# Two trunk layers on one core: the last pieces of layer 0 and the first of layer 1 taken in twos, block by block, with a third buffer for the modulation weights

## The chip, the cores and the metric

The kernel runs on one core of a Trainium2 chip, in fp32 with matmuls on fp32r halves. The metric is the time on the device in microseconds (us), the median of a few runs; lower is better.

## The reference, cut to what matters

Two layers are computed for 128 context tokens and 256 latent tokens, which share all weights. Each layer first derives a shift, a scale and a gate from a condition vector, then norms and modulates its input, projects it, mixes it, projects it back and adds it through the gate.

```python
def _rmsnorm(x, g):
    y = xf * lax.rsqrt(jnp.mean(xf * xf, axis=-1, keepdims=True) + NORM_EPS)
    ...
def _adaln(cond, w_mod, b_mod):
    m = jax.nn.silu(cond) @ w_mod + b_mod          # (2048) @ (2048, 6144)
    return jnp.split(m, 3, axis=-1)                # shift, scale, gate
def _modulate(x, norm_g, shift, scale):
    return _rmsnorm(x, norm_g) * (1.0 + scale) + shift
...
for layer in range(DEPTH):
    h_p = _modulate(y_prompt, norm_g, sh_p, sc_p)  # context tokens: c_ctx
    h_s = _modulate(y_sample, norm_g, sh_s, sc_s)  # latent tokens: c
    # layer 0: h @ l0_w_in (7680 columns), HGRN2 scans and attention, @ l0_w_out
    # layer 1: h @ l1_w_in (5120 columns), windowed attention, @ l1_w_out
    y_prompt = y_prompt + gt_p * out_p
    y_sample = y_sample + gt_s * out_s
```

## The kernel before, in words

All 384 tokens are kept on the chip as three blocks of 128: block 0 is the context, blocks 1 and 2 are the latent tokens. A fp32 product is made from halves: a value is split into a rounded part (`hi`, `hh`) and the rest (`lo`, `hl`), and three matmuls replace one (L334 to L341).

`group` multiplies one column group of a weight matrix with all tokens. It walks over the 2048 rows of the weights in pieces of 512 KB: 2 row tiles by 512 columns, or 4 by 256, so 8 or 4 pieces a group. `w_piece` loads a piece on SyncE's queue into `raw` (4 buffers, L315), ScalarE rounds it to `whi` (3 buffers, L317), and VectorE subtracts to get `wlo` (2 buffers, L319). Then TensorE runs the piece's matmuls, block of tokens by block of tokens, into one PSUM tile per block; a group with token rows has 3 blocks x row tiles x 3 matmuls. A block's sum is complete only in the last piece. After every piece, `step` runs one step of the queued work on heads, and `pump` runs some units of the modulation work.

A unit of modulation work is one row tile of `l*_w_mod`: a load of 128 x 1024 floats into `mraw` (2 buffers, SyncE's queue, L229) and two VectorE operations that add its rows, times the condition, into `acc` (L233, L235). Eight such sums run through the kernel, 16 units each, 128 units in all.

The order on each engine is fixed before the run, by a list scheduler: of the instructions that its own clock holds ready, an engine gets the one of highest priority. The order of the program is the priority, and `tc.high_priority(n)` moves instructions ahead by `n`; `w_piece` has BOOST. Engines then run their lists in order, and wait where the data is not there.

The layer change is the place where layer 0's output projection ends and layer 1's input projection begins. The output projection goes over five column groups (`COLS`): three of 512 and two of 256 columns. In each group, a block's sum is multiplied by the gate (L994), the residual is added (L997), ScalarE squares and sums it (`sum_sq`, L361), the result goes to DRAM for later (`y1d`, L999, on GpSimd's queue), and TensorE turns it to feature-major tiles (`turn_x`, L368) that ScalarE scales (L977). After the last group, `rstd_row` makes 1/rms for each block: a VectorE sum (L382) and scaling (L373), a power on GpSimd (L374), a turn on TensorE (L385) into one PSUM tile `rb1`. `modulate_scaled` then makes `h1` in four quarters of 4 row tiles: for quarter 0, row tile by row tile, VectorE multiplies by `rb1` block by block (L412, tile tE), ScalarE adds the shift and rounds (`hh`, L416), VectorE makes the rest (`hl`, L417). Quarters 1 to 3 (tiles tF, tG, tH) are made by `next_h1`, with multiplies over two row tiles and all tokens; quarter 1 ahead of layer 1's first group, quarter 2 after that group's second piece, quarter 3 after its fourth. That first group is 512 columns wide (keys, `k1`), and each of its 8 pieces uses half a quarter. In this text W0, W1, W2 are its first three pieces.

Of the kernel before, what the change touches and what calls it, by code (L numbers as in the profile page):

```python
# [14 lines left out]
P = 128  # L15
# [20 lines left out]
MRAWB = 2  # L36
# [8 lines left out]
def trunk_kernel(ctx: ExitStack, tc: tile.TileContext, I, O):  # L45
# [177 lines left out]
    def mod_acc(l, c0):  # L223

        acc = mpool.tile([P, 2, 1024], F32, tag="acc", name=nm("acc"))
        cs = csil_g[l] if c0 >= 2 * D else csil
        for kt in range(KT):
            raw = wpool.tile([P, 1024], F32, tag="mraw", bufs=MRAWB, name=nm("mraw"))
            nc.sync.dma_start(raw, I[f"l{l}_w_mod"][kt * P:kt * P + P, c0:c0 + 1024])  # L229
# [92 lines left out]
    def group(w, c0, hq, fm, after=None, n=512):  # L322

        nt = 4 if fm else 3
        nk = 1024 // n
        ps = [psm.tile([P, 512], F32, tag="mm", name=nm("mm"))[:, 0:T if fm else n] for _ in range(nt)]
        for kt in range(0, KT, nk):
            hh, hl = hq[kt // 4]
            with tc.high_priority(BOOST):
                hi, lo = w_piece(wpool, "raw", RAWB, w, kt, nk, c0, n)  # L330
            for c in range(nt):
                cs = slice(c * P, c * P + P)
                for k in range(nk):
                    kq = kt % 4 + k  # L334
                    if fm:
                        ops = ((hi[:, k, cs], hh[:, kq]), (hi[:, k, cs], hl[:, kq]), (lo[:, k, cs], hh[:, kq]))
                    else:
                        ops = ((hh[:, kq, cs], hi[:, k]), (hh[:, kq, cs], lo[:, k]), (hl[:, kq, cs], hi[:, k]))
                    for i, (a, b) in enumerate(ops):
                        nc.tensor.matmul(ps[c], lhsT=a, rhs=b, start=(kt + k == 0 and i == 0),  # L340
                                         stop=(kt + k == KT - 1 and i == 2))  # L341
# [9 lines left out]
    def group_b(w, c0, hq, n=512):  # L351
        return group(w, c0, hq, False, n=n)
# [5 lines left out]
    def sum_sq(ss, x, g):  # L358
        for b in range(3):
# [45 lines left out]
    def modulate_scaled(l, q, xt, rb, parts):  # L405

        hh, hl = hq_tiles(q)
        for k0, k1, cts in parts:
            for c, s in cts:
                x = xt[:, k0:k1, s]  # L410
                r = rb[:, s].unsqueeze(1).broadcast_to([P, k1 - k0, s.stop - s.start])
                nc.vector.tensor_tensor(out=x, in0=x, in1=r, op=ALU.mult)  # L412
            for k in range(k0, k1):
                for c, s in CT if len(cts) == 1 else cts:
# [256 lines left out]
    def start_mod(k0, k1):  # L671

        for k, nk in pairs(k0, k1):
# [18 lines left out]
            sums = small(4 * nk, "ms").rearrange("p (b c) -> p b c", c=2)  # L692
# [286 lines left out]
    COLS = [(512 * g, 512) for g in range(3)] + [(1536, 256), (1792, 256)]  # L979
    for i, (c0, n) in enumerate(COLS):  # L980
        g, o = c0 // 512, c0 % 512
        if o == 0:
            x = load_x("CD"[g % 2], g, nc.gpsimd)
        ps = group_b(I["l0_w_out"], c0, o0, n)
# [7 lines left out]
        with tc.high_priority(2 * BOOST if i == 4 else BOOST):  # L992
            for b in range(3):
                nc.vector.tensor_tensor(out=y[:, b], in0=ps[b], in1=gb[:, min(b, 1), o:o + n], op=ALU.mult)  # L994
        with tc.high_priority(2 * BOOST if i == 4 else 0):
# [6 lines left out]
        if i < 4:  # L1002
            later(0, turn)
        else:
            with tc.high_priority(2 * BOOST):
                turn()


    finish_mods()
    h1 = []  # L1010
    ALL = ((0, slice(0, T)),)
    BLOCKS = ((0, slice(0, P)), (1, slice(P, 2 * P)), (1, slice(2 * P, T)))

    def next_h1(q):
        with tc.high_priority(BOOST):
            h1.append(modulate_scaled(1, q, yT[q], rb1, ((0, 2, ALL), (2, 4, ALL))))

    with tc.high_priority(2 * BOOST):
        rb1 = rstd_row(ss1)
# [129 lines left out]
```

## Time and profile before

| what | value |
|---|---|
| median of 3 runs | 1389.26 us (1388.11 to 1390.78) |
| profiled execution, its own time | 1387.91 us |
| span in its trace | 1386.1 us |
| TensorE busy (matmuls) | 1336.0 us, 96% of the span |
| VectorE busy | 1022.0 us, 74% |
| ScalarE busy | 651.6 us, 47% |
| DMA | 265.45 MB, mean 192 GB/s |

The profile is of one execution. A matmul's end is modelled and consecutive matmuls overlap, so busy time of TensorE says little about how densely they follow each other; the distance between two starts says more. An idle time in a row is that of the engine just before the instruction, with what ended it. The granted clock is given as a share of 2.4 GHz.

### The profile page before, as it was taken

The page shows a single profiled execution, that of the slowest core. Times are in us where ns is not written, and L with a number is a line of the kernel's source. Part 1 is how long each engine was busy: PE and PEld are TensorE (multiplying, and loading weights), DVE is VectorE, ACT ScalarE, POOL GpSimd, SP SyncE. Part 2 cuts the span into 40 slices and gives each one's busy share as a digit, 9 for nine tenths or more (in the row PEclk, how much of TensorE's full clock was granted, in tenths as well). Part 3 has the DMA queues.
Part 4 walks back from the last instruction along what each step waited for, and adds up shares of the span by engine and source line. Part 5 has one row for each costly group of instructions (what it writes and reads, how often), then busy time and mean ns, then how long its engine had stood idle before and what let it go on. Part 6 is the DMA issues. An engine that isn't in the chain of part 4 may idle for free.

```text
span 1386.1 us, 19705 instructions
## 1 busy us (share of the span) xinstructions
PE 1336.0 (96%) x7381; PEld 1148.0 (83%) x7381; DVE 1022.0 (74%) x1608; ACT 651.6 (47%) x1302; POOL 80.6 (6%) x86
## 2 busy tenths in 40 slices
PE   5899999999999999999999998989999999999998
PEld 4778788987888887788977896878888899997788
DVE  6587658998996999984896357885656664488753
ACT  4532324485654545655432345434866763352221
POOL 1000000000000041101000000200000001000000
PEclk8999999999999999999999998999999999999999
DMA  9899898746554475665577542674322335457742
GB/s 285 276 347 326 289 304 288 228 128 221 162 187 133 153 226 189 212 215 168 158 237 243 180 149 88 220 250 139 105 78 91 96 113 173 132 174 224 242 163 69
DMA packets 142239, 265.45 MB, mean 192 GB/s; under 512 B 8960, under 2 KB 54976, under 8 KB 142144
## 3 DMA queue, kind: packets, MB, share of 16 engines
q1 hardware_dynamic: 136288, 245.73, 55.2%
q0 software_dynamic: 5600, 18.39, 4.4%
q8 instruction: 58, 0.95, 0.3%
q14 instruction: 37, 0.30, 0.1%
q10 hardware_dynamic: 256, 0.08, 0.0%
HBM read 256.04 MB, written 8.13 MB: 191 GB/s over the span
## 4 chain that ended last, share of the span: by engine, by line
PE 73%; DVE 12%; DMA 9%; issue 3%; POOL 1%; ACT 1%; SPq 0%; DVEq 0%; POOLq 0%; ACTq 0%
PE mm L340 49%; DMA mraw<-in_l_w_mod_dram 8%; DVE acc L235 5%; PE mm L661 4%; PE mm L663 4%; PE mm L662 4%; DVE wlo L319 3%; PE px L519 3%; PE px L682 2%; DMA raw<-in_l_w_in_dram 1%; PE px L579 1%; POOL sm L374 1%; PE px L596 1%; PE px L542 1%; PE px L368 1%
## 5 line engine op out<-in xcount | busy, mean ns | idle before, releaser
L317 ACT CAST whi<-raw 128x1024 fp32r<-128x1024 f32 (+1 forms) x270 | 278.1, 1031 | 527.6 <-PE mm L340 399.8
L319 DVE TENSOR_TENSOR wlo<-raw,whi 128x1024 fp32r<-128x1024 f32 (+1 forms) x270 | 323.6, 1199 | 190.9 <-PE mm L340 152.2
L340 PE MATMUL mm<-wlo,hh 128*128 128x512 f32 (+1 forms) x1104 | 414.3, 375 | 13.4 <-DVE wlo L319 13.4
L340 PE MATMUL mm<-whi,hh 128*128 128x512 f32 (+1 forms) x1104 | 418.3, 379 | 1.2 <-ACT hh L416 0.8
L340 PE MATMUL mm<-whi,hl 128*128 128x512 f32 (+1 forms) x1104 | 413.1, 374 | 0.0
L235 DVE SCALAR_TENSOR_TENSOR acc<-mraw,csil,acc 128x1024 f32<-128x1024 f32 x240 | 301.6, 1282 | 39.0 <-DMA mraw<-in_l_w_mod_dram 38.5
L340 PEld LDWEIGHTS mm<-wlo,hh 128*128 128x128 f32 x1104 | 209.7, 190 | 53.3 <-DVE wlo L319 19.3
L340 PEld LDWEIGHTS mm<-whi,hh 128*128 128x128 f32 x1104 | 209.4, 190 | 39.2 <-issue 1.7
L340 PEld LDWEIGHTS mm<-whi,hl 128*128 128x128 f32 x1104 | 209.6, 190 | 36.1
L661 PE MATMUL mm<-hh,whi 128*128 128x384 f32 x384 | 132.8, 352 | 7.5 <-ACT hh L401 4.4
L340 PE MATMUL mm<-hh,whi 128*128 128x384 f32 x384 | 131.5, 342 | 1.3 <-DVE tM L612 1.3
L662 PE MATMUL mm<-hl,whi 128*128 128x384 f32 x384 | 130.9, 341 | 0.1
L340 PE MATMUL mm<-hh,wlo 128*128 128x384 f32 x384 | 129.5, 337 | 0.0
L340 PE MATMUL mm<-hl,whi 128*128 128x384 f32 x384 | 129.1, 336 | 0.0
L663 PE MATMUL mm<-hh,wlo 128*128 128x384 f32 x384 | 125.2, 342 | 1.1 <-DVE wlo L319 1.1
L661 PEld LDWEIGHTS mm<-hh,whi 128*128 128x128 f32 x384 | 73.3, 192 | 21.4 <-issue 10.4
L663 PEld LDWEIGHTS mm<-hh,wlo 128*128 128x128 f32 x384 | 73.1, 192 | 3.4 <-DVE wlo L319 1.7
L340 PEld LDWEIGHTS mm<-hh,whi 128*128 128x128 f32 x384 | 72.2, 188 | 3.4 <-DVE tM L612 2.2
L662 PEld LDWEIGHTS mm<-hl,whi 128*128 128x128 f32 x384 | 73.7, 192 | 0.8 <-DVE hl L402 0.4
L340 PEld LDWEIGHTS mm<-hl,whi 128*128 128x128 f32 x384 | 72.2, 188 | 0.9
L340 PEld LDWEIGHTS mm<-hh,wlo 128*128 128x128 f32 x384 | 72.1, 188 | 0.7 <-issue 0.2
L554 ACT ACTIVATE p<-px,nb,rs 128x384 f32<-128x384 f32 (+1 forms) x72 | 42.3, 594 | 13.0 <-DVE nb L552 8.3
(445 smaller groups left out, 1404.9 us busy)
## 6 DMA issues: line engine op xcount, KB each, us to landing
raw<-in_l_w_in_dram SPq DMA_DIRECT2D x194, 512.0 KB, 4.0
mraw<-in_l_w_mod_dram SPq DMA_DIRECT2D x192, 512.0 KB, 4.9
raw<-in_l_w_out_dram SPq DMA_DIRECT2D x64, 512.0 KB, 4.4
raw<-in_l_w_in_dram SPq DMA_DIRECT2D x12, 256.0 KB, 7.2
tK<-in_l_b_mod_dram POOLq DMA_DIRECT2D x6, 256.0 KB, 5.6
y1d<-tA POOLq DMA_DIRECT2D x2, 768.0 KB, 6.5
tD<-y1d POOLq DMA_DIRECT2D x2, 768.0 KB, 6.3
tL<-y1d POOLq DMA_DIRECT2D x2, 768.0 KB, 6.7
```

The source lines that it names most:

```text
L235: nc.vector.scalar_tensor_tensor(out=acc[:, c], in0=raw, scalar=s, in1=acc[:, c], op0=ALU.mult, op1=ALU.add)
L317: nc.scalar.copy(hi, raw)
L319: nc.vector.tensor_tensor(out=lo, in0=raw, in1=hi.bitcast(F32), op=ALU.subtract)
L340: nc.tensor.matmul(ps[c], lhsT=a, rhs=b, start=(kt + k == 0 and i == 0), stop=(kt + k == KT - 1 and i == 2))
L368: nc.tensor.transpose(ps[:, b * P:b * P + P], x[:, b, k * P:k * P + P], ident)
L374: nc.gpsimd.tensor_tensor(out=out, in0=out, in1=nhalf[:, 0:out.shape[1]], op=ALU.pow)
L519: nc.tensor.matmul(out, lhsT=a, rhs=b, start=(i == 0), stop=(i == len(ops) - 1))
L554: nc.scalar.activation(p[:, j], ss[j], AF.Exp, bias=nb[:, j:j + 1], scale=rs[:, i + j:i + j + 1], accum_out=sm[:, j:j + 1])
L661: nc.tensor.matmul(ps[c][:, 0:T], lhsT=wh, rhs=hh[:, kq], start=(kt + k == k0), stop=False)
L662: nc.tensor.matmul(ps[c][:, 0:T], lhsT=wh, rhs=hl[:, kq], start=False, stop=False)
L663: nc.tensor.matmul(ps[c][:, 0:T], lhsT=wl, rhs=hh[:, kq], start=False, stop=(kt + k == k1 - 1))
L682: nc.tensor.matmul(ps[32 * (j % 4):32 * (j % 4) + 32, part * n:part * n + n], lhsT=cs32[:, kt, :], rhs=raw[:, j], start=(kt < 4), stop=(kt ...
```

## The change

The buffers of `mraw` go from 2 to 3, and `mod_acc` issues each load two units ahead of its use (one more `yield` per sum). `group` gets an argument `two`: a piece in it is held, and its matmuls are run together with those of the next piece, block by block: all of both pieces for block 0, then for block 1, then for block 2, with the products of `lo` weights last in each piece and block. It is used for the third and fourth piece of the last column group of layer 0 and for the first and second piece of layer 1. The work after a block of the last column group (gate, residual, square, norm) is made per block at a higher priority, and quarter 0 of `h1` block by block. Each block has a PSUM tile of its own for the turned norm, and ScalarE copies it to a tile in SBUF for the later quarters. The last store to `y1d` goes to SyncE's queue. A small tile (`ms`) moves to another pool.

```diff
-MRAWB = 2
+MRAWB = 3
...
 def mod_acc(l, c0):
+        raws = []
+        def load(kt):
+            raws.append(wpool.tile([P, 1024], F32, tag="mraw", bufs=MRAWB, name=nm("mraw")))
+            nc.sync.dma_start(raws[kt], I[f"l{l}_w_mod"][kt * P:kt * P + P, c0:c0 + 1024])
+        for kt in range(MRAWB - 1):
+            load(kt)
+        yield
         for kt in range(KT):
-            raw = wpool.tile([P, 1024], F32, tag="mraw", bufs=MRAWB, name=nm("mraw"))
-            nc.sync.dma_start(raw, I[f"l{l}_w_mod"][kt * P:kt * P + P, c0:c0 + 1024])
+            if kt + MRAWB <= KT:
+                load(kt + MRAWB - 1)
+            raw = raws[kt]
...
-    def group(w, c0, hq, fm, after=None, n=512):
+    def group(w, c0, hq, fm, after=None, n=512, two=()):
+        def products_of(c, kt, hi, lo):
+            ...
+            if held:
+                ops = [o for i, o in enumerate(ops) if i % 3 != 1] + ops[1::3]
+            for i, (a, b) in enumerate(ops):
+                nc.tensor.matmul(ps[c], lhsT=a, rhs=b, start=(kt == 0 and i == 0),
+                                 stop=(kt + nk == KT and i == len(ops) - 1))
+        held = []
         for kt in range(0, KT, nk):
...
+            if kt // nk in two:
+                held.append((kt, hi, lo))
+            else:
+                if held:
+                    held.append((kt, hi, lo))
+                for c in range(nt):
+                    for p in held or ((kt, hi, lo),):
+                        products_of(c, *p)
+                held.clear()
...
-            sums = small(4 * nk, "ms").rearrange("p (b c) -> p b c", c=2)
+            sums = spool.tile([P, 8], F32, tag="ms", bufs=2, name=nm("ms"))[:, 0:4 * nk].rearrange("p (b c) -> p b c", c=2)
...
+    def norm_block(b):
+        r = r1[:, b:b + 1]
+        nc.vector.tensor_reduce(out=r, in_=ss1[:, b:b + 1], axis=AX.X, op=ALU.add)
+        rpow(r, r, D, EPS)
+        ps = px()
+        nc.tensor.transpose(ps[:, 0:P], r.broadcast_to([P, P]), ident)
+        return ps[:, 0:P]
+
+    def first_h1(b, rb):
+        s, c = slice(b * P, b * P + P), min(b, 1)
+        for k in range(4):
+            x, m = yT[0][:, k, s], modc[1][:, k, c:c + 1]
+            nc.vector.tensor_tensor(out=x, in0=x, in1=rb, op=ALU.mult)
+            nc.scalar.activation(h1[0][0][:, k, s], x, AF.Identity, bias=m)
+            nc.vector.scalar_tensor_tensor(out=h1[0][1][:, k, s], in0=x, scalar=m, in1=h1[0][0][:, k, s].bitcast(F32),
+                                           op0=ALU.add, op1=ALU.subtract)
...
     for i, (c0, n) in enumerate(COLS):
+        last = i == len(COLS) - 1
-        ps = group_b(I["l0_w_out"], c0, o0, n)
+        ps = group_b(I["l0_w_out"], c0, o0, n, (2,) if last else ())
...
+        for b in range(3):
+            with tc.high_priority(3 * BOOST if last else BOOST):
                 nc.vector.tensor_tensor(out=y[:, b], in0=ps[b], in1=gb[:, min(b, 1), o:o + n], op=ALU.mult)
+            if last:
+                with tc.high_priority(3 * BOOST):
+                    nc.vector.tensor_tensor(out=y[:, b], in0=y[:, b], in1=xo[:, b], op=ALU.add)
+                    sum_sq(ss1, y, i, (b,))
+                    rb = norm_block(b)
+                with tc.high_priority(2 * BOOST):
+                    first_h1(b, rb)
+                    nc.scalar.copy(rb1[:, b * P:b * P + P], rb)
...
-        nc.gpsimd.dma_start(y1d[:, c0:c0 + n].rearrange("(b p) c -> p b c", p=P), y)
+        (nc.sync if last else nc.gpsimd).dma_start(y1d[:, c0:c0 + n].rearrange("(b p) c -> p b c", p=P), y)
...
-            with tc.high_priority(2 * BOOST):
+            with tc.high_priority(BOOST):
                 turn()
...
-    with tc.high_priority(2 * BOOST):
-        rb1 = rstd_row(ss1)
-        h1.append(modulate_scaled(1, 0, yT[0], rb1, [(k, k + 1, BLOCKS) for k in range(4)]))
...
-    evict_tm(group(W1, 2048, h1, False, lambda q: next_h1(q + 2) if q < 2 else None), k1)
+    evict_tm(group(W1, 2048, h1, False, lambda q: next_h1(q + 2) if q < 2 else None, two=(0,)), k1)
```

## Rows read from the trace of the kernel before

**Rows 1.** The page: busy time of each engine, share of the span, instructions

```profile
PE 1336.0 (96%) x7381; PEld 1148.0 (83%) x7381; DVE 1022.0 (74%) x1608; ACT 651.6 (47%) x1302; POOL 80.6 (6%) x86
```

**Rows 2.** TensorE's waits over the span: us in total, times, longest us

```profile
PE mm L340 <- DVE wlo L319: 13.4, 11, 3.2
```

**Rows 3.** VectorE's waits over the span, the same columns

```profile
DVE acc L235 <- DMA mraw<-in_l_w_mod_dram: 38.5, 35, 4.6
```

**Rows 4.** Windows: length; busy us of PE, PEld, DVE, ACT, POOL; clock; DMA share; GB/s

```profile
0.00:100.00 100.00, 78.51 (x585) 63.73 (x586) 67.00 (x128) 42.15 (x88) 4.18 (x11) 0.91 0.93 300
...
736.80:740.20 3.40, 3.38 (x8) 2.71 (x9) 2.69 (x3) 0.00 (x0) 0.00 (x0) 0.51 0.78 263
...
838.00:842.50 4.50, 4.45 (x11) 3.52 (x12) 4.45 (x19) 3.18 (x9) 0.00 (x0) 0.50 0.09 33
...
852.20:856.40 4.20, 4.18 (x11) 3.32 (x12) 4.20 (x10) 1.85 (x5) 0.00 (x0) 0.59 0.43 125
...
865.00:935.00 70.00, 66.33 (x297) 53.59 (x296) 62.11 (x59) 25.46 (x51) 9.21 (x3) 1.00 0.72 234
```

**Rows 5.** Timeline of TensorE at the layer change: start, us, line, operation [idle before]

```profile
823.18 0.28 PE L340 MATMUL mm<-whi,hl 128*128 128x256 f32 x1
...
826.06 0.28 PE L340 MATMUL mm<-whi,hl 128*128 128x256 f32 x1
...
832.82 0.28 PE L340 MATMUL mm<-whi,hl 128*128 128x256 f32 x1
...
838.05 0.80 PE L340 MATMUL mm<-whi,hh 128*128 128x512 f32 x1 [0.81 <-ACT hh L416]
...
843.03 0.40 PE L340 MATMUL mm<-whi,hh 128*128 128x512 f32 x1
...
848.25 0.39 PE L340 MATMUL mm<-whi,hl 128*128 128x512 f32 x1
...
852.22 0.51 PE L340 MATMUL mm<-wlo,hh 128*128 128x512 f32 x1 [2.90 <-DVE wlo L319]
```

**Rows 6.** Timeline of VectorE at the layer change

```profile
828.90 0.42 DVE L994 TENSOR_TENSOR tB<-mm,tM 128x256 f32<-128x256 f32 x1 [0.28 <-PE mm L340]
...
833.02 1.22 DVE L319 TENSOR_TENSOR wlo<-raw,whi 128x1024 fp32r<-128x1024 f32 x1 [0.42 <-PE mm L340]
834.16 0.42 DVE L994 TENSOR_TENSOR tB<-mm,tM 128x256 f32<-128x256 f32 x1
...
837.27 0.68 DVE L412 TENSOR_TENSOR tE<-tE,px 128x128 f32<-128x128 f32 x3 [1.26 <-PE px L385]
...
842.64 0.95 DVE L412 TENSOR_TENSOR tF<-tF,px 128x768 f32<-128x768 f32 x1
845.99 0.65 DVE L417 SCALAR_TENSOR_TENSOR hl<-tE,modc,hh 128x128 fp32r<-128x128 f32 x2 [2.40 <-ACT hh L416]
...
850.93 1.23 DVE L319 TENSOR_TENSOR wlo<-raw,whi 128x1024 fp32r<-128x1024 f32 x1
```

**Rows 7.** Timeline of SyncE's queue and of VectorE in layer 0's output projection

```profile
725.08 0.34 SPq L229 DMA_DIRECT2D mraw<-in_l_w_mod_dram  x1
...
733.15 2.48 DVE L235 SCALAR_TENSOR_TENSOR acc<-mraw,csil,acc 128x1024 f32<-128x1024 f32 x2 [4.57 <-DMA mraw<-in_l_w_mod_dram]
735.54 1.22 DVE L319 TENSOR_TENSOR wlo<-raw,whi 128x1024 fp32r<-128x1024 f32 x1
```

**Rows 8.** Group of line 385 at the layer change: xcount | busy us, mean ns

```profile
L385 PE MATMUL px<-ct,r 128*128 128x128 f32 x3 | 1.1, 374 | 1.9 <-POOL r L374 1.9
```

**Rows 9.** Timeline of GpSimd at the layer change

```profile
835.34 0.78 POOL L999 DMA_DIRECT2D y1d<-tB  x1 [2.10 <-DVE tB L997]
```

**Rows 10.** TensorE's waits from 17 to 215 us

```profile
PE px L682 <- DMA mraw<-in_l_w_mod_dram: 6.0, 3, 4.7
```

**Rows 11.** DMA issues, 0 to 100 us, then 865 to 935 us: count, KB each, median us to landing

```profile
mraw<-in_l_w_mod_dram SPq DMA_DIRECT2D x40, 512.0 KB, 7.5
...
mraw<-in_l_w_mod_dram SPq DMA_DIRECT2D x16, 512.0 KB, 4.7
```

More of the change, by code (lines that the diff above doesn't have):

```diff
@@ L326, in group @@
         ps = [psm.tile([P, 512], F32, tag="mm", name=nm("mm"))[:, 0:T if fm else n] for _ in range(nt)]
+        def products_of(c, kt, hi, lo):
+            hh, hl = hq[kt // 4]
+            cs = slice(c * P, c * P + P)
+            ops = []
+            for k in range(nk):
+                kq = kt % 4 + k
+                if fm:
+                    ops += ((hi[:, k, cs], hh[:, kq]), (hi[:, k, cs], hl[:, kq]), (lo[:, k, cs], hh[:, kq]))
+                else:
+                    ops += ((hh[:, kq, cs], hi[:, k]), (hh[:, kq, cs], lo[:, k]), (hl[:, kq, cs], hi[:, k]))
+            if held:
[4 more added lines that the diff above has]
+        held = []
         for kt in range(0, KT, nk):
-            hh, hl = hq[kt // 4]
             with tc.high_priority(BOOST):
                 hi, lo = w_piece(wpool, "raw", RAWB, w, kt, nk, c0, n)
[L331 to L341, printed above, removed]
+            if kt // nk in two:
+                held.append((kt, hi, lo))
+            else:
+                if held:
[4 more added lines that the diff above has]
+                held.clear()
             step()
@@ L349, in group_a, with group_b, sum_sq @@
         return group(w, c0, hq, True, after)
-    def group_b(w, c0, hq, n=512):
-        return group(w, c0, hq, False, n=n)
+    def group_b(w, c0, hq, n=512, two=()):
+        return group(w, c0, hq, False, n=n, two=two)
     def hq_tiles(q):
         return [hpool.tile([P, 4, T], F32R, tag=f"h{s}{q}", name=nm(f"h{s}{q}")) for s in ("h", "l")]
-    def sum_sq(ss, x, g):
-        for b in range(3):
+    def sum_sq(ss, x, g, blocks=range(3)):
+        for b in blocks:
             junk = mpool.tile([P, 512], F32, tag="t2", bufs=T2B, name=nm("junk"))
@@ L407, in modulate_scaled @@
         hh, hl = hq_tiles(q)
[L408 to L412, printed above, removed]
+        for k0, k1 in parts:
+            x = xt[:, k0:k1]
+            r = rb.unsqueeze(1).broadcast_to([P, k1 - k0, T])
+            nc.vector.tensor_tensor(out=x, in0=x, in1=r, op=ALU.mult)
             for k in range(k0, k1):
-                for c, s in CT if len(cts) == 1 else cts:
+                for c, s in CT:
                     b = modc[l][:, 4 * q + k, c:c + 1]
@@ L991, in trunk_kernel @@
         y, xo = y4[:, :, o:o + n], x[:, :, o:o + n]
-        with tc.high_priority(2 * BOOST if i == 4 else BOOST):
-            for b in range(3):
-                nc.vector.tensor_tensor(out=y[:, b], in0=ps[b], in1=gb[:, min(b, 1), o:o + n], op=ALU.mult)
-        with tc.high_priority(2 * BOOST if i == 4 else 0):
+        if last:
+            finish_mods()
+            rb1 = t6("L")[:, 0:T]
+            h1.append(hq_tiles(0))
+        for b in range(3):
+            with tc.high_priority(3 * BOOST if last else BOOST):
+                nc.vector.tensor_tensor(out=y[:, b], in0=ps[b], in1=gb[:, min(b, 1), o:o + n], op=ALU.mult)
+            if last:
+                with tc.high_priority(3 * BOOST):
[5 more added lines that the diff above has]
+                    nc.scalar.copy(rb1[:, b * P:b * P + P], rb)
+        if not last:
             for b in range(3):
```

10 lines of the change are left out of this document (4 added, 6 removed).

## The prediction

> **What bounds the kernel now.** I read the page first. TensorE's matmuls are busy for 1336.0 of 1386.1 us, VectorE for 1022.0 us, no other engine comes near [rows 1]. So the kernel is bound by TensorE nearly everywhere, and what can be won is the time in which TensorE waits or runs at half clock. An edit that only speeds another engine is worth what it takes from those waits.
>
> The second view is the list of TensorE's waits. Its largest entry is the one for the weights' low half: 13.4 us in 11 waits [rows 2]. The third view, VectorE's waits, says what makes `wlo` late: VectorE runs in a fixed order and stands 38.5 us, in 35 waits, before an `acc` operation whose `mraw` load has not landed [rows 3]. A `wlo` behind such an operation waits with it. The timeline shows one case whole: the load is issued at 725.08, `acc` starts at 733.15 after 4.57 us of waiting, the `wlo` behind it at 735.54 [rows 7], and TensorE, which had to stand still, then runs 3.40 us at half of 2.4 GHz [rows 4].
>
> The other large hole is the layer change. The last matmul of layer 0 starts at 832.82 and lasts to 833.1; layer 1's first one starts at 838.05 and at 1.2 GHz; W2 waits 2.90 us more for its `wlo` and starts at 852.22, again at low clock [rows 4, 5]. In these 19.1 us between 833.1 and 852.22, W0 and W1 needed only 36 matmuls. At full clock one takes (848.25 - 843.03) / 23 = 0.227 us [rows 5], so 8.2 us.
>
> **The layer change, step by step.** The sum runs along VectorE, since it is what W2 waited for.
>
> Taking two pieces together moves no work: the last two pieces of layer 0 hold 72 matmuls in either order, and end at the same 833.1. But block 0 and block 1 are complete earlier. A block is 24 of the 72 matmuls; 24 of 256 columns took 826.06 - 823.18 = 2.9 us [rows 5]. So block 0 is ready 5.8 us and block 1 2.9 us before the end, where before block 0 was evicted at 828.90 [rows 6], 4.2 us ahead of it. From a block's eviction to its first multiply by 1/rms it takes 837.27 - 834.16 = 3.1 us [rows 6]. So block 0's quarter is made while TensorE still works on layer 0, block 1's partly too, and only block 2's chain stays behind the end.
>
> For block 2: eviction at 833.1 instead of 834.16 (its priority is now above that of the `wlo` that stood ahead of it from 833.02 [rows 6]), first multiply at 836.2. Quarter 0 before was 24 operations of VectorE, of which 22 ran from 837.27 to 842.64, 0.244 us each [rows 6]; the 8 of block 2 take 1.95 us, to 838.2. Behind them VectorE has the same work as before: from 842.64 to the end of W2's `wlo` at 850.93 + 1.23 it was 9.5 us, of which 2.40 were a wait for ScalarE and 0.65 were left over from quarter 0 [rows 6], so 6.4 us of work. That gives W2's `wlo` at 844.6 and **7.6 us won** against 852.22. The low clock ahead of W2 is kept in this sum, since TensorE would still stand there: W0 and W1 end at 833.1 + 8.2 + 1.8 (three turns of 0.374 [rows 8], and an estimate of 0.7 for the six turns of the last columns, which are pipelined) = 843.1.
>
> The bounds: if VectorE makes W2's `wlo` in time, TensorE alone sets the end, 843.1, and the low clock behind 852.22 goes too (4.20 us at 0.59, so 1.7 us [rows 4]): 10.8 us won. If the wait of 2.40 for ScalarE comes back and one `wlo` of 1.22 stands ahead of block 2's chain again [rows 6], 4.0 us are won.
>
> Costs taken as nothing: the three copies of the norm on ScalarE (it waits for VectorE's results in this stretch and holds 2.40 us of slack [rows 6]; without it some 0.25 us each, an estimate from VectorE's 128-column operations [rows 6]); the last store on SyncE's queue (behind it are loads for pieces whose buffers come free only as TensorE goes on; GpSimd loses an issue of 0.78 us [rows 9]). Both `wlo` buffers are held until the third block's share of W0 is done. W2's `wlo` can so begin only at 833.1 + 1.8 + 5.5 + 1.4 = 841.8, which is still ahead of the 843.4 (844.6 - 1.23) at which VectorE comes to it; if that cover goes, it is rival 2. The other quarters' multiplies now read the norm from SBUF, at no price that a row shows.
>
> **The third `mraw` buffer.** Each load can now be issued one unit earlier, and a unit is two `acc` operations, 2.48 us [rows 7]. The waits are 1.1 us in the mean and 4.6 at most [rows 3], so taken one by one nearly all would go. What they cost TensorE: 13.4 us less the 2.9 at the layer change [rows 2, 5], and half of the 3.40 us at low clock [rows 4], 12.2 us in all. That is the upper bound; the lower is nothing. I take 8, since the lead is larger than most waits, but the scheduler will use the third buffer to pack the units closer, and the loads then meet more traffic. In 0 to 100 us, at 300 GB/s, a load lands after 7.5 us; in 865 to 935, at 234 GB/s, after 4.7 [rows 4, 11]. The page "DMA: Bandwidth & Descriptors" of the Trainium skill (§ Issuing engines are not separate DMA queues) says that all queues run on the same 16 engines and interleave. By it a third load in flight buys no bandwidth and only slows the others, which is rival 1; the trace agrees as far as landing times grow with traffic.
>
> **The start.** There the same edit costs. The DMA engines are 0.93 busy, and TensorE waits 6.0 us for the start's own weight loads, 4.7 at once [rows 4, 10]. One more load of 512 KB ahead of them is 1.75 us at 300 GB/s [rows 4]. I take 1.5; the bounds are 0 and 1.75. The extra `yield` moves a unit by one place in the order and adds no instruction.
>
> **Sum.** 7.6 + 8 - 1.5 = 14.1 us. Against the profiled execution's 1387.91 that is 1373.8; this execution is 1.35 us below the median of the runs, so the forecast is 1375. By the bounds the gain lies between 4.0 + 0 - 1.75 = 2.3 and 10.8 + 12.2 = 23.0 us, so from 1366.3 to 1387.0.
>
> **The rivals.**
>
> 1. The third buffer wins nothing: units are packed closer until loads are late by as much as now. For it speaks that units already run as fast as their loads come, 0.72 busy on the DMA engines [rows 4]; against it that 234 GB/s is well below the 300 of the start. Time: 1389.3 - 7.6 + 1.5 = 1383.
> 2. The wait at W2 stays, because both `wlo` buffers are held through two pieces. If W2's `wlo` then again comes 7.8 us after W0's share ends (W0 ended at about 844.4: 11 matmuls to 842.5 or so [rows 4] and 7 more at 0.227 to 0.43; the `wlo` ended at 852.16 [rows 6]), it ends at 849.6 and only 2.6 us are won there. Time: 1389.3 - 2.6 - 8 + 1.5 = 1380.
> 3. Slower. With data early, the scheduler puts `acc` operations ahead of `wlo` in stretches where TensorE has no slack. One such operation is about 1.24 us (2.48 for two [rows 7]). In one of ten of the 128 units it would cost 16 us and give 1389.3 - 7.6 + 1.5 + 16 = 1399. It decides the sign from one unit in 26 on, where it eats the 6.1 us that the other two terms leave. Against it: `wlo` has the higher priority, and must be kept out by an operation already running.
> 4. Both bounds at once: nothing of the waits is left. Time: 1389.3 - 10.8 - 12.2 + 1.5 = 1368.
>
> **How the numbers follow.** A difference of 0.2%, 2.8 us, is about what a measurement of this kernel tells from none. My forecast has 0.45, with a range of its own from 1370 to 1380; rival 1 has 0.16, rival 2 0.11, rival 3 0.08, rival 4 0.12, and 0.08 is left for a change under 0.2%, where the start loses more and the layer change wins its least. Faster is 0.45 + 0.16 + 0.11 + 0.12 = 0.84, the same 0.08, slower 0.08. The range that leaves out no more than 2 in 10 cuts rival 3 and half of the small cases: 1366 to 1386.
>
> **What the profile after would show.** Right: the first 512-column matmul of layer 1 follows layer 0's last 256-column one within about 2 us; W2 starts some 11.5 us after layer 0's last matmul, not 19.1; VectorE's waits for `mraw` fall from 38.5 us to under 15, and TensorE's for `wlo` to under 6; no low clock near 737 us. Wrong: W2's `wlo` still the longest wait at the layer change (rival 2), waits for `mraw` as long as before with later landings (rival 1), or `wlo` with no wait of its own but starting behind `acc` operations while TensorE idles (rival 3). The sum fails if a wait in the start grows by more than the 1.75 us allowed.

## The result, and the profile after

The change takes 1374.78 us (median of 4 runs, 1370.95 to 1375.27), against 1390.02 us (4 runs, 1388.11 to 1392.46) for the kernel before on the same chip: a ratio of 0.9883, 95% interval 0.9859 to 0.9908. In a second comparison, with 6 runs of the same kernel against 11 of before, the ratio was 0.9908 (0.9890 to 0.9927). Both intervals lie below 1: the change is about 1% faster. The profiled execution took 1375.27 us with a span of 1373.5 us, 12.6 us less than before.

The page's row of busy times, of the change:

```profile
PE 1332.6 (97%) x7381; PEld 1145.3 (83%) x7381; DVE 1019.1 (74%) x1608; ACT 651.0 (47%) x1305; POOL 72.3 (5%) x85
```

Work is the same as in [rows 1], with ScalarE's three new copies. So the gain must lie in waits and in TensorE's clock. TensorE's waits for `wlo` and VectorE's for `mraw`, over the span of the change (us in total, times, longest):

```profile
PE mm L354 <- DVE wlo L330: 5.9, 4, 2.9
...
DVE acc L246 <- DMA mraw<-in_l_w_mod_dram: 11.2, 5, 4.4
```

Before they were 13.4 us in 11 waits [rows 2] and 38.5 us in 35 [rows 3].

To place the gain, the table below counts matmuls. Both kernels run the same 5616 matmuls of the weights' column groups in the same groups. The column `before` is the start of the n-th of them in us, and the others are how much earlier (-) or later (+) the n-th starts in the profile of that kernel. A difference between two lines of a column is what that stretch won or lost. The layer change lies between 3168 and 3330. Each column is one execution; e1 to e12 are the experiments below, and e9 is the change itself again.

```
   n  before  change     e1     e2     e3     e4     e5     e6     e7     e8     e9    e10    e11    e12
 192    84.4    -0.2   -1.5   -2.5   -0.7   +1.4   -1.7   -0.3   +1.1   -1.3   +0.6   -0.6   +1.0   -0.8
1152   294.2    +0.3   -2.3   -2.3   -1.2   +2.4   -1.6   -0.4   +1.8   -0.9   +0.6   -0.5   +0.3   +3.1
1344   340.6    +0.7   -2.3   -1.9   -0.8  +10.3   -1.3   -0.1   +2.2   -0.6   +1.0   -0.1   +0.6   +3.5
1536   404.6    +1.0   -1.6   -1.5   +3.0   +9.7   -0.9   +0.3   +2.5   -0.2   +1.3   +0.3   +4.4   +3.8
2688   718.5    +0.5   -1.1   -2.6   +1.4   +8.4   -1.4   -1.1   +1.4   -0.7   +0.9   -0.4   +2.5   +3.3
3168   820.1    -2.2   +0.5   -5.4   -0.8   +6.5   -3.8   -3.8   -2.2   -2.9   -2.7   -3.6   +0.5   +0.4
3330   860.1    -8.0   -5.4   -6.1   -0.6   +0.8   -8.7   -8.1  -10.2   -7.2   -8.3  -11.6   -6.0   -5.4
3648   939.1   -13.1   -8.5  -11.2   -5.7   -4.3  -13.8  -13.2  -15.3  -12.3  -13.4  -16.7  -11.0  -10.5
4500  1173.5   -13.0   -8.5  -11.2   -5.6   -4.2  -13.8  -13.2  -15.3  -12.2  -13.3  -16.7  -11.0  -10.5
5270  1332.2   -16.2   -6.9  -14.4   -8.8   -7.4  -17.0  -16.4  -18.5  -13.3  -16.6  -17.7  -14.2  -13.7
5400  1356.1   -12.7   -6.9  -12.3   -8.8   -7.4  -14.9  -14.4  -16.4  -15.4  -14.5  -19.9  -14.2  -11.6
5615  1381.9   -12.7   -6.9  -12.3   -8.8   -7.4  -14.9  -14.4  -16.4  -15.4  -14.5  -19.9  -14.2  -11.6
```

In the change: +0.5 up to 718 us, -2.7 around the stall of [rows 7], -5.8 at the layer change, -5.1 in the stretch behind it, -3.2 between 1173 and 1332 us, and then +3.5, a loss that the prediction didn't have. They add up to the -12.7 of the last line. The windows of the change that belong to it (length; busy us of PE, PEld, DVE, ACT, POOL; clock; DMA share; GB/s):

```profile
0.00:100.00 100.00, 79.81 (x592) 63.80 (x593) 70.30 (x132) 42.87 (x88) 4.21 (x11) 0.95 0.96 309
736.80:740.20 3.40, 1.91 (x9) 1.38 (x8) 3.40 (x4) 1.04 (x1) 0.00 (x0) 1.00 0.32 120
839.00:842.30 3.30, 0.41 (x2) 0.00 (x0) 3.30 (x9) 2.51 (x6) 0.00 (x0) 0.98 0.00 0
842.15:845.60 3.45, 3.25 (x8) 2.57 (x9) 3.45 (x8) 2.44 (x5) 0.00 (x0) 0.51 0.53 153
855.00:930.00 75.00, 75.00 (x341) 62.34 (x340) 68.17 (x70) 30.87 (x60) 3.53 (x3) 1.00 0.76 246
1337.10:1340.50 3.40, 3.40 (x18) 3.40 (x18) 2.66 (x5) 0.00 (x0) 0.00 (x0) 0.50 0.33 128
```

The second and the fifth answer to [rows 4]: no low clock at 737 us in this execution, and TensorE busy without a gap from 855 to 930 us, at 246 GB/s, where it had gaps at 234. The third shows what is left of the layer change: TensorE idles while VectorE is busy throughout. The fourth and the sixth are 3.4 us each at half clock.

**The layer change after.** The timeline of TensorE, for [rows 5]:

```profile
829.82 0.64 PE L354 MATMUL mm<-wlo,hh 128*128 128x256 f32 x4
830.29 0.40 PE L354 MATMUL mm<-whi,hh 128*128 128x512 f32 x1
...
839.02 0.40 PE L354 MATMUL mm<-whi,hl 128*128 128x512 f32 x1
842.35 2.92 PE L354 MATMUL mm<-wlo,hh 128*128 128x512 f32 x6 [2.94 <-DVE wlo L330]
845.08 1.09 PE L354 MATMUL mm<-whi,hh 128*128 128x512 f32 x3
```

Layer 1's first 512-column matmul follows layer 0's last at once. 30 of the 36 matmuls of W0 and W1 are out by 839.02. The last six, the products with W1's low half, wait 2.94 us and then run at half clock; W2 starts behind them at 845.08. The timeline of VectorE, for [rows 6], says why they wait:

```profile
826.78 0.68 DVE L1021 TENSOR_TENSOR tE<-tE,px 128x128 f32<-128x128 f32 x3 [1.14 <-PE px L1013]
...
829.20 1.22 DVE L330 TENSOR_TENSOR wlo<-raw,whi 128x1024 fp32r<-128x1024 f32 x1
...
830.50 0.42 DVE L1047 TENSOR_TENSOR tB<-mm,tM 128x256 f32<-128x256 f32 x1
...
832.07 0.68 DVE L1021 TENSOR_TENSOR tE<-tE,px 128x128 f32<-128x128 f32 x3 [0.50 <-PE px L1013]
...
834.17 0.69 DVE L1021 TENSOR_TENSOR tE<-tE,px 128x128 f32<-128x128 f32 x3 [0.56 <-PE px L1013]
834.77 0.77 DVE L1023 SCALAR_TENSOR_TENSOR hl<-tE,modc,hh 128x128 fp32r<-128x128 f32 x2
...
835.65 1.14 DVE L1023 SCALAR_TENSOR_TENSOR hl<-tE,modc,hh 128x128 fp32r<-128x128 f32 x4
836.71 1.82 DVE L439 TENSOR_TENSOR tF<-tF,tL 128x768 f32<-128x768 f32 x2
838.44 2.72 DVE L444 SCALAR_TENSOR_TENSOR hl<-tF,modc,hh 128x128 fp32r<-128x128 f32 x8
841.08 1.22 DVE L330 TENSOR_TENSOR wlo<-raw,whi 128x1024 fp32r<-128x1024 f32 x1
...
843.08 1.22 DVE L330 TENSOR_TENSOR wlo<-raw,whi 128x1024 fp32r<-128x1024 f32 x1
```

`wlo` at 829.20 is W0's, at 841.08 W1's, at 843.08 W2's; 830.50 is the eviction of block 2. The first multiplies by 1/rms are at 826.78 for block 0, 832.07 for block 1 and 834.17 for block 2; the two `hl` at 834.77 are the last of block 1. All of quarter 1 (tF: two multiplies, eight `hl`, 4.4 us) stands ahead of W1's. Both have the priority BOOST, and quarter 1's code comes first in the program.

**The stall near 733 us after.** VectorE's timeline, for [rows 7]; below it TensorE's, and last TensorE's wait at this place in the kernel before:

```profile
736.09 1.28 DVE L246 SCALAR_TENSOR_TENSOR acc<-mraw,csil,acc 128x1024 f32<-128x1024 f32 x1 [4.39 <-DMA mraw<-in_l_w_mod_dram]
737.29 1.22 DVE L330 TENSOR_TENSOR wlo<-raw,whi 128x1024 fp32r<-128x1024 f32 x1
```

```profile
738.56 0.50 PE L354 MATMUL mm<-wlo,hh 128*128 128x512 f32 x1 [1.49 <-DVE wlo L330]
```

```profile
736.82 0.79 PE L340 MATMUL mm<-wlo,hh 128*128 128x512 f32 x1 [3.17 <-DVE wlo L319]
```

`acc` waits nearly as long here as before, since the units ahead of it ran earlier too: from 722 to 732 us VectorE starts six `acc` operations, against three before. But TensorE waits 1.49 us where it waited 3.17, and keeps its clock. That is not so in every execution: in e5 and e8, whose code is the same up to here, TensorE waits 1.82 and 2.05 us at this place, and the granted clock behind it is 0.50 for some 3.4 us.

**The end.** TensorE's timeline of the change between 1334 and 1337 us:

```profile
1334.25 0.50 PE L288 MATMUL px<-ahi,ones_r 128*128 128x512 f32 x1 [0.21 <-ACT ahi L285]
1335.43 0.51 PE L289 MATMUL px<-alo,ones_r 128*128 128x512 f32 x1 [0.67 <-DVE alo L287]
1336.22 0.39 PE L354 MATMUL mm<-whi,hh 128*128 128x256 f32 x1 [0.29 <-DVE t L1141]
```

L288 and L289 make gates of the last projection from a finished `acc`. A column group's result can't be evicted without its gate, so here the next group's first matmul, at 1336.22, waits for the eviction (`t`, L1141), and the low clock of the sixth window follows. With before's order there was no loss here; that the gates were late because of the change is shown by e4 and e8.

### The profile page after: what moved, and what is told of

It is laid out like the page before. It is cut to its first block, busy times and chain, and to the rows that moved or that the text cites. A ratio compares the mean times of both kernels' runs of the same rounds, so it can differ in the third digit from the quotient of the medians.

```text
span 1373.5 us, 19691 instructions
## 1 busy us (share of the span) xinstructions
PE 1332.6 (97%) x7381; PEld 1145.3 (83%) x7381; DVE 1019.1 (74%) x1608; ACT 651.0 (47%) x1305; POOL 72.3 (5%) x85
## 4 chain that ended last, share of the span: by engine, by line
PE 69%; DVE 6%; ACT 1%; issue 1%; DMA 1%; POOL 0%; DVEq 0%; POOLq 0%; ACTq 0%
PE mm L354 58%; PE px L546 3%; DVE wlo L330 2%; DVE acc L246 2%; PE px L606 1%; PE px L623 1%; PE px L569 1%; PE px L861 1%; DMA mraw<-in_l_w_mod_dram 1%; PE px L864 1%; DMA tab<-in_l_b_qnorm_dram 0%; PE px L536 0%; PE px L878 0%; PE px L868 0%; PE px L396 0%
## 5 line engine op out<-in xcount | busy, mean ns | idle before, releaser
L354 PE MATMUL mm<-wlo,hh 128*128 128x512 f32 (+1 forms) x1104 | 408.5, 374 | 6.0 <-DVE wlo L330 5.9
L246 DVE SCALAR_TENSOR_TENSOR acc<-mraw,csil,acc 128x1024 f32<-128x1024 f32 x240 | 299.7, 1277 | 11.3 <-DMA mraw<-in_l_w_mod_dram 11.2
```

The source lines that it names most:

```text
L246: nc.vector.scalar_tensor_tensor(out=acc[:, c], in0=raw, scalar=s, in1=acc[:, c], op0=ALU.mult, op1=ALU.add)
L354: nc.tensor.matmul(ps[c], lhsT=a, rhs=b, start=(kt == 0 and i == 0), stop=(kt + nk == KT and i == len(ops) - 1))
```

## The experiments

Twelve runs, in three batches that each have a kernel before of their own on the same chip (medians 1386.50, 1388.02 and 1387.76 us). Ratios are to that one, with 95% intervals.

**e1: the layer change alone.** The changed kernel with two `mraw` buffers and the loads as before:

```diff
-MRAWB = 3
+MRAWB = 2
...
-        for kt in range(MRAWB - 1):
-            load(kt)
-        yield
...
```

> The change without its loads: two mraw buffers, each load issued in the unit that uses it, no extra yield. Theory: the layer change alone wins 5.5 to 7.6 us (the matmuls of the two traces stand 5.7 us closer behind it), so about 1383 to 1384.5 where the kernel before has 1390; VectorE's waits for mraw stay near 38 us and the stalls of TensorE near 733, 902 to 931 and 1276 to 1296 us come back. Rival: the layer change needs the early loads too, and wins under 2 us alone.

Measured: 1378.52 us, 0.9940 (0.9916 to 0.9963). The layer change wins 5.9 us in the table, as in the change. VectorE's waits for `mraw` in e1:

```profile
DVE acc L235 <- DMA mraw<-in_l_w_mod_dram: 40.3, 37, 5.5
```

So nothing at the layer change needs the third buffer, and nothing at the layer change shortens the waits for `mraw`. The stretch behind, 3330 to 3648, wins 3.1 us even here, against 5.1 with the buffer: what e1 and e2 win there doesn't simply add.

**e2: the loads alone.** The kernel before with the new `mod_acc` (loads two units ahead, the extra `yield`), three buffers and the move of `ms`:

```diff
-MRAWB = 2
+MRAWB = 3
...
+        for kt in range(MRAWB - 1):
+            load(kt)
+        yield
...
```

> The kernel before with the loads of the change: three mraw buffers, loads two units ahead, the extra yield. Theory: the waits for mraw fall from 38.5 to about 11 us, which wins 11 us, and 3.6 us are given back in the last groups, where the gates are made one unit later: about 1382 to 1384. Rival: the third buffer only packs units closer, waits stay above 25 us, and the time is within 2 us of before.

Measured: 1380.03 us, 0.9945 (0.9924 to 0.9966). VectorE's waits in e2:

```profile
DVE acc L246 <- DMA mraw<-in_l_w_mod_dram: 12.7, 5, 4.3
```

The stalls near 733, behind the layer change and before 1332 us go (-2.8, -5.1 and -3.2 in the table), and 2.1 us are lost between 5270 and 5400. The gains of e1 and e2 at their medians are 8.0 and 6.5 us, together 14.5; the change wins 15.2 in its own comparison, and 13.9 as e9.

**e3: the third buffer, loads in the old order.** The kernel before with MRAWB = 3 and `ms` moved, and nothing else.

> The kernel before with three mraw buffers and nothing else: loads are written in the unit that uses them, no extra yield. If the buffer count does the work, the waits fall to about 11 to 15 us and the time to about 1379 to 1381, below the loads alone, since the gates of the last groups are not late. If issuing ahead in the order does it, the waits stay above 25 us and less than 4 us are won.

Measured: 1377.09 us, 0.9921 (0.9893 to 0.9949). VectorE's waits in e3:

```profile
DVE acc L235 <- DMA mraw<-in_l_w_mod_dram: 8.6, 5, 4.6
```

It is the buffer that takes the waits away; issuing each load two units ahead in the program adds nothing to that. Between 5270 and 5400 e3 loses nothing. It loses 3.8 us between 1344 and 1536 instead; see e4.

**e4: no extra yield.** The changed kernel, the two loads of a sum's start in the same step as its first unit:

```diff
             load(kt)
-        yield
         for kt in range(KT):
```

> The change without the one yield that stands ahead of each sum; loads still run two units ahead. Theory: with it each sum ends one unit later, which at 0.6 units a piece is 1.7 pieces or 7 us; the last gates then meet the end of their column group, and TensorE waits there and falls to half clock. Without it those 3.6 us come back: about 1371 where the change has 1375, with no low clock near 1340 us. Rival: the late gates come from something else, and the time stays within 1 us of the change.

Measured: 1378.33 us, 0.9941 (0.9919 to 0.9963), slower than the change at the median. In the table the end behaves as was expected: 5270 to 5400 loses 0.0, where every kernel with the extra yield and the old pace loses 2.0 to 3.5. But 7.9 us are lost between 1152 and 1344, which no theory had. The windows of that stretch, first in e4 and then in the change; both start near matmul 1150 and are 26 us long:

```profile
296.00:322.00 26.00, 20.85 (x86) 15.22 (x84) 14.50 (x30) 24.98 (x30) 0.00 (x0) 0.93 0.28 81
```

```profile
292.00:318.00 26.00, 26.00 (x122) 21.02 (x121) 19.91 (x38) 20.55 (x26) 0.00 (x0) 1.00 0.40 123
```

ScalarE, the fourth engine in the row, is busy for 24.98 of 26 us in e4, and TensorE runs 86 matmuls where it runs 122 in the change. The timeline of ScalarE in e4 shows with what:

```profile
299.55 1.28 ACT L820 ACT_TABLE_LOAD   x1
300.85 0.52 ACT L820 ACTIVATE hg<-tA 128x384 f32<-128x384 f32 x1
301.39 1.28 ACT L781 ACT_TABLE_LOAD   x1
302.69 0.71 ACT L781 ACTIVATE tE<-tB,ct,lb 128x384 f32<-128x384 f32 x1
303.41 1.28 ACT L821 ACT_TABLE_LOAD   x1
```

L820 and L821 are exponentials, L781 is a logarithm. Taking the one `yield` out shifted the steps of queued work against each other, the scheduler's list for ScalarE alternates between the two functions, and each turn costs a table load of 1.28 us. Over the whole run there are 17 such loads in e4, 15 in e3 and e11, and 9 in before, the change and all the others. It takes both, the third buffer and the missing `yield`: before and e1, with two buffers and no `yield`, have 9. The page "ScalarE: Activation LUTs" of the Trainium skill (§ Table sets: the hidden batching unit) says that a logarithm and an exponential share a table set and need one load between them; the trace doesn't agree, in these rows each pays one.

**e5: no pairs.** The changed kernel without `two`, so that pieces are taken one by one; the work per block stays:

```diff
-        ps = group_b(I["l0_w_out"], c0, o0, n, (2,) if last else ())
+        ps = group_b(I["l0_w_out"], c0, o0, n)
...
-    evict_tm(group(W1, 2048, h1, False, lambda q: next_h1(q + 2) if q < 2 else None, two=(0,)), k1)
+    evict_tm(group(W1, 2048, h1, False, lambda q: next_h1(q + 2) if q < 2 else None), k1)
```

> The change with no piece held: norm and first quarter still per block, pieces one by one. Theory: the pairs bring most of the 5.6 us of the layer change, since without them blocks 0 and 1 are complete 2.9 and 1.4 us before the end and not 5.8 and 2.9: the matmuls behind the layer change stand 3 to 4.5 us later than in the change, about 1378 to 1379. Rival: making the norm per block at a higher priority is what wins, and the loss is under 1.5 us.

Measured: 1376.48 us, 0.9910 (0.9889 to 0.9931). The layer change wins 4.9 us, against 5.8 with the pairs. So the pairs are worth about 1 us of it, and not most of it as was expected; norm, first quarter and evictions made per block at a higher priority bring the rest. No run parts the work per block from its priority.

**e6: W0's and W1's halves first.** The changed kernel with the weight pieces of the first pair at a higher priority, ahead of quarter 1:

```diff
-            with tc.high_priority(BOOST):
+            with tc.high_priority(2 * BOOST if 0 in two and kt // nk < 2 else BOOST):
                 hi, lo = w_piece(wpool, "raw", RAWB, w, kt, nk, c0, n)
```

> The change with the loading and splitting of layer 1's first two pieces at the priority of the first quarter, so ahead of quarter 1. The trace of the change shows that TensorE's wait of 2.9 us at 839 us is for the low half of the second piece (W1), which VectorE makes after ten operations of quarter 1. Theory: that wait and the low clock behind it go; the wait moves to W2, which comes at 843.6 where it came at 845.1: 1.5 to 4 us less, about 1371 to 1373. Rival: quarter 1 is then late by as much, and the matmuls behind the layer change stand within 0.7 us of the change.

Measured: 1375.03 us, 0.9904 (0.9886 to 0.9922). The timeline of VectorE in e6, and below it the wait that TensorE has:

```profile
835.16 1.22 DVE L330 TENSOR_TENSOR wlo<-raw,whi 128x1024 fp32r<-128x1024 f32 x1
836.30 1.82 DVE L439 TENSOR_TENSOR tF<-tF,tL 128x768 f32<-128x768 f32 x2
838.04 2.80 DVE L444 SCALAR_TENSOR_TENSOR hl<-tF,modc,hh 128x128 fp32r<-128x128 f32 x8
...
841.63 1.22 DVE L330 TENSOR_TENSOR wlo<-raw,whi 128x1024 fp32r<-128x1024 f32 x1
```

```profile
842.90 0.80 PE L354 MATMUL mm<-wlo,hh 128*128 128x512 f32 x1 [3.02 <-DVE wlo L330]
```

W1's low half comes at 835.16 instead of 841.08 (e6 is 1.6 us ahead of the change at matmul 3168), and nothing is won: the wait is as long and stands one piece later, at W2. The layer change wins 4.3 us here, less than in the change, but that is not the order's doing: e8 has the change's own code at this place and wins 4.3 us too. Its wait for W1's low half is 2.99 us, as in the change (2.94). What differs from the change is the clock behind the wait, here in e8:

```profile
841.05:847.85 6.80, 6.15 (x15) 4.80 (x16) 6.80 (x13) 3.93 (x9) 0.00 (x0) 0.50 0.55 154
```

e6 runs at the same 0.50 from 842.1 to 848.9 us. Both so have 6.8 us at half clock, where the change has 3.45. So the change's code at the layer change wins 5.6 to 5.9 us in five executions (change, e1, e4, e9, e12) and 4.3 in one, and 1.4 us of a difference there can be the clock alone.

**e7: W2's halves first too.** As e6, with `< 3` for `< 2`.

> As the run before, with W2 too. Theory: W2's low half is made as soon as a buffer is free, about 840, and TensorE waits less than 1.5 us in all between layer 0's last matmul and W3: 3 to 5 us less than the change, about 1370 to 1372. Rival: VectorE then stands before the buffer of W2 while quarter 1 is due, and nothing is won over the run before.

Measured: 1370.92 us, 0.9867 (0.9844 to 0.9890). The layer change wins 8.0 us, 2.2 more than in the change. The timeline of VectorE in e7:

```profile
836.78 1.22 DVE L330 TENSOR_TENSOR wlo<-raw,whi 128x1024 fp32r<-128x1024 f32 x1
837.91 0.95 DVE L439 TENSOR_TENSOR tF<-tF,tL 128x768 f32<-128x768 f32 x1
838.78 1.22 DVE L330 TENSOR_TENSOR wlo<-raw,whi 128x1024 fp32r<-128x1024 f32 x1
839.92 1.40 DVE L444 SCALAR_TENSOR_TENSOR hl<-tF,modc,hh 128x128 fp32r<-128x128 f32 x4
```

Both low halves come before the second half of quarter 1, and the two multiplies of quarter 1 no longer run back to back. A wait of 2.19 us is left, at W3 (847.74), 0.75 us shorter than the change's. VectorE works without a gap from 834.24 us up to it, so what remains is VectorE's work itself. The clock stays up behind the wait:

```profile
830.00:860.00 30.00, 27.34 (x124) 21.59 (x123) 28.53 (x65) 20.28 (x51) 1.19 (x2) 1.00 0.47 137
```

So only part of the 2.2 us is the order. e10 and e11 below have the same order and the same wait (2.19 and 2.17 us): e10 keeps its clock and wins 8.0 us as well; e11 has a granted clock of 0.50 from 850.8 to 854.2 us and wins 6.5. With as much low clock as in the change, the order is so worth some 0.7 us; the other 1.5 are the half clock that did not follow in e7 and e10.

**e8: a faster pace for the last projection.** The changed kernel with more units of modulation work per piece at the end:

```diff
-RATE3 = 0.6
+RATE3 = 0.75
```

> The change with 0.75 units a piece in layer 1's output projection where it has 0.6. The last sum's gates come some 17 units in; at 0.6 that is 28 pieces, at 0.75 it is 23. Theory: the 3.6 us lost between 1316 and 1341 us are due to the gates being made one unit later, at the end of their column group; made earlier they cost nothing, and everything ahead of 1217 us stays as in the change: about 3.6 us less, 1371. Rival: the loss is not tied to when the gates are made, and stays.

Measured: 1372.95 us, 0.9889 (0.9872 to 0.9906). The window of its end, in e8:

```profile
1329.00:1340.00 11.00, 11.00 (x82) 10.45 (x81) 6.59 (x9) 2.33 (x3) 0.00 (x0) 1.00 0.58 199
```

No gap and no low clock there: 5270 to 5400 wins 2.1 us, where the change loses 3.5. Of the 3.2 us that the change wins in the stretch ahead, 4500 to 5270, 1.1 are left. Over both stretches e8 wins 3.2 us, and the change loses 0.3 (e9, the same code again, wins 1.2). So the gates were late by the one unit that the extra yield put them back, and the term is real in the trace; the total is not told apart from the change's by its interval.

**e9: the change itself, e10: e7 and e8 together, e11: e7 with the old load order** (three buffers, no yield), run in one batch.

> The change itself, on the chip of the next three runs, so that they can be compared with it. Expected as measured before: a ratio of 0.986 to 0.991 to the kernel before, and the same waits stage by stage.

> The change with layer 1's first three pieces first (2.3 us less at the layer change) and 0.75 units a piece in the last projection (3.6 us less there). Theory: the two places do not touch each other, so both gains add: 5 to 6 us less than the change on the same chip, a ratio of about 0.995 to 0.996 to it. Rival: the later stage gives back what the earlier one wins, and the sum is under 3 us.

> The change with layer 1's first three pieces first, three mraw buffers, but loads written in the unit that uses them and no extra yield. Theory: the buffer count, not the order of the loads, keeps VectorE from waiting, so its waits for mraw stay at 8 to 13 us; the last gates are made one unit earlier and the stall of 3.6 us near 1335 us is gone. At the layer change 2.3 us less as before. Without the yield the stages from 300 to 410 us can come out 4 to 9 us worse, as in two runs above. So 1369 if they don't, 1375 if they do. Rival: waits for mraw rise above 20 us without the early loads.

Measured: e9 1373.87 us, 0.9908 (0.9890 to 0.9927); e10 1372.32 us, 0.9887 (0.9868 to 0.9906); e11 1369.40 us, 0.9876 (0.9856 to 0.9895). In the table both gains of e10 stand side by side, and its profiled execution ends 5.4 us ahead of e9's; its median is only 1.5 us lower. Whether they add in the mean is open. e11 loses the same 3.8 us between 1344 and 1536 as e3, with the same 15 table loads, and still has the lowest median: 4.5 us under e9 on the same chip. The intervals of e11 and e9 overlap, and so do those of e7 and the change; but each of these ratios has the scatter of a kernel before in it. Run by run, five of e11's six times lie below all six of e9, and all four of e7, from another batch on the same chip, do too. Against that, e10 has e7's edit and a median of 1372.32 us. That e7's order or e11 beats the change is likely and not shown.

e9's loss between 5270 and 5400 is 2.1 us, against 3.5 in the change's first profile, with the same code. TensorE has the same three waits there as in the change (0.21, 0.67 and 0.29 us), 0.33 us earlier. The window of e9 that answers to the sixth one above:

```profile
1337.10:1340.50 3.40, 3.40 (x31) 3.40 (x30) 3.28 (x5) 0.83 (x1) 0.00 (x0) 1.00 0.43 164
```

The clock did not fall in that execution. So the late gates cost 2.1 us, and the low clock, where it follows, 1.4 more.

**e12: the last store on GpSimd's queue as before.**

```diff
-        (nc.sync if last else nc.gpsimd).dma_start(y1d[:, c0:c0 + n].rearrange("(b p) c -> p b c", p=P), y)
+        nc.gpsimd.dma_start(y1d[:, c0:c0 + n].rearrange("(b p) c -> p b c", p=P), y)
```

> The change with the last store of layer 0's result on GpSimd's queue, as it was. Theory: the queue makes no difference, since GpSimd's issue of 0.78 us falls between two powers and SyncE's loads are not waited for: within 1 us of the change, and the matmuls behind the layer change stand within 0.5 us. Rival: the issue stands ahead of the third block's power and makes the layer change 0.7 us or more longer.

Measured: 1373.63 us, 0.9907 (0.9887 to 0.9926), and 5.8 us at the layer change: close to e9 in both (0.9908 and 5.6). The store's queue is worth nothing that a run shows.

## Why the prediction was right, and where its terms were not

**The layer change: 7.6 predicted, 5.8 measured, a term that was too large.** The mechanism was as described in the main: block 0's first quarter is made under layer 0's last matmuls. Two steps failed. The first is "only block 2's chain stays behind the end". Block 1 is evicted at 827.80, but its first multiply comes at 832.07, 1.6 us behind layer 0's last matmul, and two of its `hl` stand at 834.77 between block 2's operations; the last `hl` of block 0 comes at 830.90. The second, and the larger one, is "Behind them VectorE has the same work as before". The operation that ran at 833.02 before [rows 6] was W1's `wlo`. The prediction moved block 2's eviction ahead of it, and did not put the operation back anywhere; it now stands at 841.08, inside the chain that ends with W2's. By the rows of VectorE above, the chain from layer 0's last matmul (829.82 + 0.64 = 830.46) takes 3.7 us to block 2's first multiply (3.1 predicted), 2.6 for the rest of quarter 0 until 836.8 (2.0), and 7.5 from there to the end of W2's `wlo` at 844.3 (6.4): 13.8 instead of 11.5. W1's `wlo` is the 1.1 of the last part; the other 1.2 are the operations of blocks 0 and 1 that the sum had under layer 0's matmuls. W2 itself starts later still, 14.6 us behind layer 0's last matmul, because "W0 and W1 end at 833.1 + 8.2 + 1.8" took W1's low half as there: its six products come late and at half clock. Against 19.1 before, that is 4.5 us at W2; the rest of the 5.8 lies ahead of and behind it, where the low clock of 852.22 [rows 4] is gone. e6 and e7 bear the account out. In e6 the same work, with W1's half ahead of quarter 1, ends as late (13.9 us behind layer 0's last matmul), and the wait stands at W2. In e7 the second half of quarter 1 is behind W2's half, and the wait falls to 2.19 us; of the 8.0 that it wins, 1.5 hang on the clock (e11: 6.5).

Rival 2 (the wait at W2 stays because both `wlo` buffers are held) did not come, though a wait for a low half is the longest one left. It is W1's, and not for a buffer: W1's buffer was free when TensorE had finished layer 0, and in e6 and e7, with the same buffers, the operation comes 4 us and more earlier by its priority alone.

That "taking two pieces together" makes the blocks complete earlier is right, and matters little: e5 keeps 4.9 of the 5.8 us without it. The prediction put the gain on the pairs; the runs put it on the work per block at a higher priority.

**The third buffer: 8 predicted, 11.0 measured.** The stretches with stalls won 2.7 + 5.1 + 3.2 = 11.0 us, near the upper bound of 12.2: the lead covered more of the waits than was allowed for. e2, e3 and e4, which share the buffer, all win 5.1 and 3.2 in the last two. Of the 5.1, e1 has 3.1 without the buffer, and e2 and e3 have all of it without the layer change: what either wins there, the other can't win again. The first stretch varies from 1.9 to 3.6 us in the kernels with the buffer. The waits for `mraw` came under the 15 us that were named (11.2), those for `wlo` just under the 6 (5.9). The low clock near 737 us is gone in the change and e9; in e5 and e8, with the same code there, it came back.

**"The extra `yield` ... adds no instruction", costed at nothing: wrong by 2.0 to 3.5 us at the end.** It adds none, but it puts each sum back by one unit, and a piece runs 0.6 units, so the last gates come 1 / 0.6 = 1.7 pieces later, where the last groups wait for them. Every kernel with the yield at the old pace loses 2.0 us or more there (change, e2, e5, e6, e7, e9, e12), the four without it lose 0.0 (e1, e3, e4, e11), and the two with the faster pace win 2.1 (e8, e10). In the traces the same `yield` also keeps away the 3.8 to 7.9 us of table loads that the kernels with three buffers and without it have (e3, e4, e11); that was not priced either.

**The start: a loss of 1.5 predicted, none measured beyond the scatter.** At matmul 1152 the change stands at +0.3, and other kernels with the third buffer between -2.3 and +3.1. TensorE's waits of the change from 17 to 100 us, with those for `hh` and for `mraw`, against [rows 10], and below them the wait for `hh` of the kernel before:

```profile
PE mm L688 <- ACT hh L429: 5.1, 2, 4.4
...
PE px L709 <- DMA mraw<-in_l_w_mod_dram: 1.7, 2, 0.9
```

```profile
PE mm L661 <- ACT hh L401: 4.4, 2, 3.4
```

The wait for the start's own loads (`mraw` in this row) went from 6.0 to 1.7 us, where the prediction had it grow; the one for `hh` grew by 0.7. The loads of this name in 0 to 100 us, of the start and of the modulation work together, against [rows 11]:

```profile
mraw<-in_l_w_mod_dram SPq DMA_DIRECT2D x41, 512.0 KB, 7.1
```

**Rival 1 (the third buffer wins nothing) is out.** Waits for `mraw` fell to a third or less in every kernel with three buffers, and loads in the start landed after 7.1 us, not later than the 7.5 before (behind the layer change after 4.7 in both). The page "DMA: Bandwidth & Descriptors" of the Trainium skill (§ Issuing engines are not separate DMA queues) says that transfers of all queues share 16 engines; no run here speaks against that. Behind the layer change the engines moved 246 GB/s, against 309 at the start, so there was room for the third load. The rival's mechanism, units packed closer until a load is late again, is seen once, near 733 us, with 4.39 us of waiting. **Rival 3** (slower, `acc` ahead of `wlo`) and **rival 4** (both bounds) did not come.

So that the forecast of 1375 met the 1374.8 us is luck in part. Errors cancelled: the layer change gave 1.8 us less than its term, the stalls 3.0 more, the start lost 1.0 less, and the gates took 3.5. And the two profiled executions are 12.6 us apart, the medians 15.2 and 13.9, with 14.1 forecast: the scatter of such a difference is as large as the errors of the terms.

## What to carry to other kernels

When the wait for one operation goes, write down the order of all operations on the engine behind it, and ask of each consumer in turn when its own input comes; pricing only the wait that was the longest before leaves out the one that takes its place. Where a step is put back by one place in a paced order, follow it to the last thing that is due: it costs nothing where there is slack, and all of it at the end. Where instruction lists come from a scheduler, an edit of one line may reorder an engine far away, so compare the start of the n-th matmul over the whole run before a difference in the total is put down to the edit, and look at the granted clock of a stretch before a difference there is.

## What was not expected of the hardware

A wait of 2.94 us was followed by 3.45 us at a granted clock of 0.51 (842.35 us), one of 3.17 us before the change by the 3.40 us at 0.51 of [rows 4], and one of 1.49 us by none (738.56 us, clock 1.00). But the length of a wait alone does not tell what follows. After the wait of 2.19 us at W3 the clock stayed at 1.00 in e7 and e10; after one of 2.17 us at the same place in e11 it was 0.50 for 3.4 us. After 2.94 us in the change it was low for 3.45 us, after 2.99 us at the same place in e8 for 6.8. One and the same stall so cost 1.4 to 1.5 us more in one execution than in another.

The same kernel on the same chip varied more from run to run than most of the effects that were looked for: before took 1380.21 to 1393.73 us in 14 runs of one batch. A switch of the function on ScalarE took 1.30 us from the load's start to that of the operation behind it (299.55 to 300.85 us), and ten of them between 295 and 318 us in e4 turned an engine that is 47% busy over the run into the one that TensorE waits for.
